# Joining the last two stores of a matmul with RMS norm into one, from one wide tile

## The chip, the cores and the metric

The kernel runs on one core of a Trainium2 chip. The metric is the device time of one execution in microseconds (us), as the median over runs; smaller is better. Beside the total I use a second figure, **the tail**: the time from the start of the last reciprocal (the instant when the last row block's 1/rms is being made) to the end of the profiled span. Times "after r" in this document are counted from the start of that reciprocal. The profile's pages round to 0.01 or 0.1 us; where I give the end of a packet or the landing of a store after r, it is from the trace's records of single packets and semaphore updates.

Three words recur. A store is *issued* by an instruction on SP or ACT; the 16 DMA engines then move it in *packets*, here one for each contiguous piece of a row; it has *landed* when its last semaphore update arrives. A run counts as "fast" unless it lies 1.5% above the fastest of the same kernel.

## The reference

```python
def reference(a, b, gamma, eps):            # a, b: 2048 x 2048 fp32, gamma: 2048
    x = np.matmul(a, b)
    rms = np.sqrt(np.mean(x ** 2, axis=-1, keepdims=True) + eps)
    return (gamma * x / rms).astype(np.float32)
```

A row of the output can only be finished when the whole row of the product is there, for rms needs its sum of squares.

## The kernel before

The kernel computes the product in bf16 and fp16 with Strassen's seven products per pair of row blocks. A row block has 128 rows, a row four chunks of `CH` = 512 columns (2 KB each in fp32); `HALF` is 1024, `N` and `K` are 2048. The last pair of row blocks is `ra`, `rb`; the part that matters here is the end of `last_group`, where block `rb` is finished. DVE is VectorE, ACT ScalarE, SP the engine that only issues here.

```python
        right = a_pool.tile([P, K], FP32, name="a32")[:, 0:HALF]
        add(right[:, 0:CH], p4[1], gam[2], ALU.mult)      # chunk 2 times gamma, out of PSUM (DVE)
        add(x22[0], seed, gam[1], ALU.mult)               # chunk 1 times gamma; x22[0] is xb[:, CH:]
        # [...] the last 16 matmuls (chunk 3 in two halves), their squares, the sum of squares
        r_b = inverse_rms(half_sq[:, 1:2], part)          # ACT: square root, DVE: reciprocal
        nc.vector.tensor_scalar_mul(out=xb[:, 0:CH], in0=xb[:, 0:CH], scalar1=r_b)   # chunk 0
        nc.sync.dma_start(out=rows(rb, 0, CH), in_=xb[:, 0:CH])
        by_r(right[:, 0:CH], r_b)                         # chunk 2, on ACT
        for bank, col in zip(half, halves):               # chunk 3, on DVE, out of PSUM
            scaled_gamma(right[:, CH:][:, col], bank, r_b, gam[3][:, col])
        nc.sync.dma_start(out=rows(rb, HALF, N), in_=right)        # chunks 2 and 3: 512 KB
        by_r(xb[:, CH:], r_b)                             # chunk 1, on ACT
        nc.scalar.dma_start(out=rows(rb, CH, HALF), in_=xb[:, CH:])   # chunk 1: 256 KB
```

So block `rb` leaves in three stores: chunk 0 early, then chunks 2 and 3 from SP's queue in rows of 4 KB, and chunk 1 from ACT's queue in rows of 2 KB.

Of the kernel before, what the change touches and what calls it, by code (L numbers as in the profile page):

```python
# [8 lines left out]
FP32 = mybir.dt.float32  # L9
# [4 lines left out]
ALU = mybir.AluOpType  # L14
# [3 lines left out]
def kernel(  # L18
# [13 lines left out]
    nc = tc.nc  # L32
    P = 128
    M, K = a.shape
    _, N = b.shape
# [4 lines left out]
    CH = 512  # L40
    NCH = N // CH
    HALF = N // 2
# [6 lines left out]
    a_pool = ctx.enter_context(tc.tile_pool(name="a_pool", bufs=2))  # L49
# [42 lines left out]
    for h, queue in enumerate((nc.sync, nc.scalar)):  # L92
        queue.dma_start(out=a0f[:, 2 * h:2 * h + 2, :],
                        in_=a[2 * h * P:(2 * h + 2) * P, 0:W2].rearrange("(r p) k -> p r k", p=P))
# [16 lines left out]
    a32 = {}  # L111
# [201 lines left out]
    def x_tile(mb, h):  # L313


        if (mb, h) not in x_half:
            n = n_x[0]
            n_x[0] += 1
            if n < 8:
                slot = n  # L320
            else:
                g = n // 4
                slot = ((0, 4, 1, 5), (0, 1, 4, 5))[g // 2 % 2 == 0][n % 4] + 2 * (g % 2)
            x_half[mb, h] = x_slot[slot]
        return x_half[mb, h]

    def x_chunk(mb, c):
        return x_tile(mb, c // 2)[:, (c % 2) * CH:(c % 2 + 1) * CH]
# [26 lines left out]
    def inverse_rms(last, partial):  # L355
        return inverse(root(last, partial))

    def rows(mb, lo, hi):
        return out[mb * P:(mb + 1) * P, lo:hi]
# [159 lines left out]
    x11, x12, x21, x22 = (x_chunk(r, c) for r in (r2, r3) for c in (2, 3))  # L519
# [185 lines left out]
    def last_group():  # L705
# [3 lines left out]
        ra, rb = 2 * g, 2 * g + 1  # L709
        x11, x12, x21, x22 = ([x_chunk(mb, 2 * j + c) for j in range(2)]  # L710
                              for mb in (ra, rb) for c in range(2))
        xa, xb = x_tile(ra, 0), x_tile(rb, 0)
        gam = [gamma_sb[:, c * CH:(c + 1) * CH] for c in range(NCH)]
# [3 lines left out]
        def partial(mb):  # L717

            m = msq[mb]
            part = stat_pool.tile([P, 1], FP32, name="part")  # L720
            nc.vector.tensor_scalar(out=part, in0=m[:, 0:1], scalar1=m[:, 1:2],
                                    scalar2=m[:, NCH:], op0=ALU.add, op1=ALU.add)
            return part
# [6 lines left out]
        def add(out, in0, in1, op=ALU.add):  # L730
            nc.vector.tensor_tensor(out=out, in0=in0, in1=in1, op=op)  # L731

        def scaled_gamma(x, src, r, gamma_of_x):
            nc.vector.scalar_tensor_tensor(out=x, in0=src, scalar=r, in1=gamma_of_x,
                                           op0=ALU.mult, op1=ALU.mult)

        def by_r(x, r):
            nc.scalar.activation(out=x, in_=x, func=ACTF.Copy, scale=r)  # L738

        p4 = []  # L740
        for j in range(2):
# [22 lines left out]
            if j == 0:  # L764
# [3 lines left out]
                seed = p7  # L768
# [19 lines left out]
        nc.sync.dma_start(out=rows(ra, CH, HALF), in_=mid)  # L788
        square(rb, seed)
        pre_b = partial(rb)  # L790
        right = a_pool.tile([P, K], FP32, name="a32")[:, 0:HALF]
        add(right[:, 0:CH], p4[1], gam[2], ALU.mult)
        add(x22[0], seed, gam[1], ALU.mult)

        half_sq = stat_pool.tile([P, 2], FP32, name="n2")
        part = stat_pool.tile([P, 1], FP32, name="part")
# [10 lines left out]
        r_b = inverse_rms(half_sq[:, 1:2], part)  # L807
        nc.vector.tensor_scalar_mul(out=xb[:, 0:CH], in0=xb[:, 0:CH], scalar1=r_b)
        nc.sync.dma_start(out=rows(rb, 0, CH), in_=xb[:, 0:CH])
        by_r(right[:, 0:CH], r_b)  # L810
        for bank, col in zip(half, halves):
            scaled_gamma(right[:, CH:][:, col], bank, r_b, gam[3][:, col])
        nc.sync.dma_start(out=rows(rb, HALF, N), in_=right)
        by_r(xb[:, CH:], r_b)
        nc.scalar.dma_start(out=rows(rb, CH, HALF), in_=xb[:, CH:])

    for g in range(G0, NG - 1):
        for j in range(2):
            group_half(g, j, hooks_of(g, j))
    last_group()  # L820

# [33 lines left out]
```

## Time and profile before

| | before |
|---|---|
| time, median of the first 3 runs | 221.2 us (221.19 to 221.22) |
| span of the profiled run | 219.0 us |
| end of the last matmul | 211.96 us |
| start of the last reciprocal | 212.89 us |
| tail, from there to the end of the span | 6.11 us |

TensorE is busy for 95% of the span, nearly to its end, and the tail is a chain of its own: reciprocal, scaling, issue, transfer, confirmation, closing waits. Only the tail can answer to this change. The lines are shown and read in the prediction below.

### The profile page before, as it was taken

Reading aid. Unit: us, or ns where it says so; the run is one execution under the profiler, and the core shown is the slowest. Engines: PE = TensorE matmul, PEld = TensorE weight load, DVE = VectorE, ACT = ScalarE, POOL = GpSimd, SP = SyncE. Lnnn points to the kernel's source line nnn. Section 1 sums busy time; section 2 is a strip of 40 time slices with the busy share of each in tenths; the row PEclk is TensorE's granted clock in tenths of the full one; section 3 lists DMA queues with packets and bytes.
Section 4 is the critical chain, followed back from the end, with each engine's and each line's share of the span. In section 5 each row is a group of like instructions: output and inputs, shape, how many; then the busy total and the mean of one; then the engine's idle time right before and its main releaser. Section 6 shows DMA issues by size and latency. Waiting matters only on the chain.

```text
span 219.0 us, 3023 instructions
## 1 busy us (share of the span) xinstructions
PE 208.8 (95%) x1012; PEld 98.4 (45%) x1032; DVE 165.9 (76%) x326; ACT 127.0 (58%) x263; POOL 36.2 (17%) x75
## 2 busy tenths in 40 slices
PE   7999999999999999999999999999999999999970
PEld 3544544444455444444444444444444444444440
DVE  1228799999899998988794649856794759787781
ACT  2110002920599898788646996289747996334471
POOL 7644433433020002100200002000200000000040
PEclk9999999999999999999999999999999999999996
DMA  7999999999939698939899049955799349145045
GB/s 152 175 202 206 204 206 209 210 208 224 414 91 332 232 278 214 379 153 263 213 294 381 19 87 272 355 233 96 174 291 396 57 89 365 69 178 208 1 179 206
DMA packets 36864, 46.60 MB, mean 213 GB/s; under 512 B 22256, under 2 KB 26352, under 8 KB 35568
## 3 DMA queue, kind: packets, MB, share of 16 engines
q0 software_dynamic: 10608, 23.86, 44.3%
q1 hardware_dynamic: 25824, 22.02, 33.4%
q10 hardware_dynamic: 416, 0.52, 0.7%
q8 instruction: 8, 0.13, 0.2%
q14 instruction: 8, 0.07, 0.1%
HBM read 34.60 MB, written 16.78 MB: 235 GB/s over the span
## 4 chain that ended last, share of the span: by engine, by line
PE 91%; DMA 3%; issue 1%; ACT 1%; POOL 1%; DVE 0%; ACTq 0%; POOLq 0%
PE acc L285 71%; PE acc L388 16%; DMA early<-in_a_dram 3%; PE tbank L419 2%; PE tbank L168 2%; PE acc L799 1%; POOL b L102 0%; PE tbank L185 0%; PE acc L185 0%; ACT x L738 0%; DVE head_at L173 0%; ACT sq L802 0%; ACT rms L352 0%; POOL t_left masks.py:199 0%; POOL t_left masks.py:197 0%
## 5 line engine op out<-in xcount | busy, mean ns | idle before, releaser
L285 PE MATMUL acc<-b,s 128*128 128x512 bf16 x397 | 92.7, 379 | 0.7
L285 PEld LDWEIGHTS <-s 128*128 128x128 f16 (+1 forms) x512 | 50.0, 98 | 59.6 <-DVE s L260 0.2
L388 PE MATMUL acc<-b,head_at 128*128 128x512 bf16 x171 | 42.2, 379 | 0.4 <-DMA b<-in_b_dram 0.3
L303 ACT ACTIVATE sq<-x 128x512 bf16<-128x512 f32 x53 | 33.4, 630 | 6.9 <-DVE x L731 3.0
L370 DVE SCALAR_TENSOR_TENSOR x<-x,r,gamma_sb 128x1024 f32<-128x1024 f32 x28 | 34.9, 1281 | 0.7
L219 ACT ACTIVATE sq<-a 128x1024 bf16<-128x1024 f32 x24 | 25.3, 1053 | 2.0 <-DMA a<-in_a_dram 1.4
L388 PEld LDWEIGHTS <-head_at 128*128 128x128 bf16 x176 | 16.9, 98 | 19.5 <-issue 0.7
L242 ACT ACTIVATE head_at<-a,s 128x2048 f16<-128x2048 f32 x10 | 20.0, 1998 | 3.4 <-DVE s L229 3.3
L102 POOL DMA_DIRECT2D b<-in_b_dram x32 | 17.2, 540 | 20.4 <-DMA b<-in_b_dram 14.1
L430 ACT COPY x<-acc 128x512 f32<-128x512 f32 x5 | 2.9, 582 | 24.6 <-PE acc L388 24.6
L285 PEld LDWEIGHTS <-head_at 128*128 128x128 f16 (+1 forms) x112 | 11.0, 98 | 13.2
L285 PEld LDWEIGHTS <-at_even 128*128 128x128 f16 x96 | 9.4, 98 | 11.3
L285 PE MATMUL acc<-early,head_at 128*128 128x512 bf16 x63 | 14.4, 379 | 0.1
L285 PE MATMUL acc<-early,s 128*128 128x512 bf16 x56 | 14.2, 379 | 0.0
L260 DVE TENSOR_TENSOR s<-head_at 128x1024 f16<-128x1024 f16 (+5 forms) x22 | 13.4, 636 | 0.1
L615 DVE TENSOR_TENSOR x<-x,x 128x512 f32<-128x512 f32 x9 | 6.2, 692 | 8.8 <-ACT x L613 8.3
L127 POOL COPY pace<-x 128x1 f32<-128x1 f32 x4 | 1.7, 413 | 66.3 <-DVE x L624 65.0
L597 ACT COPY x<-acc 128x512 f32<-128x512 f32 x9 | 5.2, 573 | 11.5 <-PE acc L285 7.7
L285 PE MATMUL acc<-t_left,s 128*128 128x512 bf16 x47 | 11.3, 379 | 0.1
L783 POOL TENSOR_SCALAR x<-x,r 128x512 f32<-128x512 f32 x1 | 2.7, 2653 | 51.2 <-DVE r L346 51.2
L276 DVE TENSOR_TENSOR b<-b 128x1024 bf16<-128x1024 bf16 x16 | 10.8, 686 | 0.2
L173 DVE COPY head_at<-tbank 128x1024 bf16<-128x1024 bf16 x7 | 4.8, 692 | 8.0 <-PE tbank L168 7.9
(113 smaller groups left out, 239.3 us busy)
## 6 DMA issues: line engine op xcount, KB each, us to landing
out_dram<-x SPq DMA_DIRECT2D x29, 512.0 KB, 3.7
a<-in_a_dram POOLq DMA_DIRECT2D x10, 1024.0 KB, 8.6
b<-in_b_dram POOLq DMA_DIRECT2D x32, 256.0 KB, 9.9
a<-in_a_dram POOLq DMA_DIRECT2D x4, 512.0 KB, 9.8
early<-in_a_dram POOLq DMA_DIRECT2D x7, 256.0 KB, 10.0
gamma_sb<-in_gamma_dram POOLq DMA_DIRECT2D x2, 512.0 KB, 8.3
out_dram<-x SPq DMA_DIRECT2D x3, 256.0 KB, 2.6
out_dram<-a SPq DMA_DIRECT2D x1, 512.0 KB, 3.3
```

What stands on the lines that cost most here:

```text
L102: nc.gpsimd.dma_start(out=raw[j][kp][:, t, :], in_=b[lo:lo + P, j * HALF:(j + 1) * HALF])
L173: nc.vector.tensor_copy(out=head_at[:, 2 * kp:2 * kp + 2, :, :], in_=view)
L219: nc.scalar.activation(out=junk, in_=a32[mb][:, h * HALF:(h + 1) * HALF], func=ACTF.Square, scale=2.0 ** -8, accum_out=n2[:, h:h + 1])
L242: nc.scalar.activation(out=a16[mb], in_=a32.pop(mb), func=ACTF.Copy, scale=factor.pop(mb))
L260: nc.vector.tensor_tensor(out=sum_of(g, s)[:, lo:hi, :], in0=x[:, lo:hi, :], in1=y[:, lo:hi, :], op=op)
L276: nc.vector.tensor_tensor(out=flat[:, 1:3, :], in0=flat[:, 1:3, :], in1=flat[:, 0::3, :], op=ALU.add)
L285: nc.tensor.matmul(bank, lhsT[:, kp, :], rhs, start=(start and kp == 0), stop=(kp == KP - 1), skip_group_check=not start)
L303: nc.scalar.activation(out=sq[:, 0:CH], in_=src, func=ACTF.Square, scale=inv_sqrt_n, accum_out=msq[mb][:, c:c + 1])
L370: nc.vector.scalar_tensor_tensor(out=x, in0=x, scalar=inverse_of[mb], in1=gamma_sb[:, h * HALF:(h + 1) * HALF], op0=ALU.mult, op1=ALU.mult)
L388: nc.tensor.matmul(bank, head_at[:, kt, r, :], head_rhs(c, kt), start=(kt == 0), stop=(kt == KT - 1))
L597: nc.scalar.copy(out=c, in_=one[1])
L615: nc.vector.tensor_tensor(out=t, in0=t, in1=x12, op=ALU.add)
```

## The change

The intent: chunk 1's product with gamma goes into the same wide tile as chunks 2 and 3, side by side with them, so that the three leave together as one store of 768 KB, each row a single packet of 6 KB. One issue, one semaphore and half of the packets are saved.

```diff
-        right = a_pool.tile([P, K], FP32, name="a32")[:, 0:HALF]
-        add(right[:, 0:CH], p4[1], gam[2], ALU.mult)
-        add(x22[0], seed, gam[1], ALU.mult)
+        wide = a_pool.tile([P, K], FP32, name="a32")
+        chunk = [wide[:, c * CH:(c + 1) * CH] for c in range(NCH)]
+        add(chunk[2], p4[1], gam[2], ALU.mult)
+        add(chunk[1], seed, gam[1], ALU.mult)
 [...]
-        by_r(right[:, 0:CH], r_b)
+        for c in (2, 1):
+            by_r(chunk[c], r_b)
         for bank, col in zip(half, halves):
-            scaled_gamma(right[:, CH:][:, col], bank, r_b, gam[3][:, col])
-        nc.sync.dma_start(out=rows(rb, HALF, N), in_=right)
-        by_r(xb[:, CH:], r_b)
-        nc.scalar.dma_start(out=rows(rb, CH, HALF), in_=xb[:, CH:])
+            scaled_gamma(chunk[3][:, col], bank, r_b, gam[3][:, col])
+        nc.sync.dma_start(out=rows(rb, CH, N), in_=wide[:, CH:])
```

## The prediction

> **What bounds the kernel now.** I read the page first: the chain that ended last, then the timeline of the last ten microseconds, the DMA issues there, and that stretch cut into windows, in this order.
>
> The chain that ended last, as shares of the span by engine:
>
> ```profile
> PE 91%; DMA 3%; issue 1%; ACT 1%; POOL 1%; DVE 0%; ACTq 0%; POOLq 0%
> ```
>
> Nine tenths of the 219.0 us span are TensorE (PE) work, one matmul after the other. The change touches no matmul, so this part stays. What it touches is the tail behind the last matmul, which ends at 211.97. The timeline there (start, duration, engine, line, operation, count; SPq and ACTq are DMA issues by the two queues):
>
> ```profile
> 212.89 0.16 DVE L346 RECIPROCAL r<-rms 128x1 f32<-128x1 f32 x1 [0.50 <-ACT rms L352]
> 213.08 0.72 ACT L738 ACTIVATE a<-a,r 128x512 f32<-128x512 f32 x1 [0.23 <-DVE r L346]
> 213.09 0.49 DVE L808 TENSOR_SCALAR x<-x,r 128x512 f32<-128x512 f32 x1
> 213.49 0.87 DVE L734 SCALAR_TENSOR_TENSOR a<-acc,r,gamma_sb 128x256 f32<-128x256 f32 x2
> 213.60 0.33 SPq L809 DMA_DIRECT2D out_dram<-x  x1
> 213.71 0.70 ACT L738 ACTIVATE x<-x,r 128x512 f32<-128x512 f32 x1
> 214.42 0.33 SPq L813 DMA_DIRECT2D out_dram<-a  x1
> 214.45 0.36 ACTq L815 DMA_DIRECT2D out_dram<-x  x1
> ```
>
> The reader is to see four chunks of 512 columns being multiplied by 1/rms (`r`), which is there at 213.05. DVE does chunk 0 (until 213.58), which is stored at once by L809. Then DVE does chunk 3 in two halves, until 213.49 + 0.87 = 214.36. ACT does chunk 2 (until 213.80) and then chunk 1 (until 214.41). Chunks 2 and 3 go out together from SP at 214.42 (L813, 512 KB), chunk 1 from ACT's queue at 214.45 (L815, 256 KB). **Both last stores leave within 0.03 us of each other.** No compute instruction follows.
>
> What follows is pure transfer. The DMA issues of the last eleven microseconds, with the median time from issue to landing, are:
>
> ```profile
> out_dram<-a SPq DMA_DIRECT2D x1, 512.0 KB, 3.3
> out_dram<-x ACTq DMA_DIRECT2D x1, 256.0 KB, 3.5
> ```
>
> So L813 lands at about 214.42 + 3.3 = 217.7 and L815 at 214.45 + 3.5 = 217.95; the second ends the kernel's work, and some 1.05 us of closing waits on SP bring the span to 219.0. The windows show what the DMA engines did (busy columns, then granted clock, DMA share, GB/s):
>
> ```profile
> 214.50:215.00 0.50, 0.00 (x0) 0.00 (x0) 0.00 (x0) 0.00 (x0) 0.00 (x0) 0.92 1.00 381
> 215.00:215.50 0.50, 0.00 (x0) 0.00 (x0) 0.00 (x0) 0.00 (x0) 0.00 (x0) 0.50 0.87 316
> 215.50:216.00 0.50, 0.00 (x0) 0.00 (x0) 0.00 (x0) 0.00 (x0) 0.00 (x0) 0.50 0.97 381
> 216.00:216.50 0.50, 0.00 (x0) 0.00 (x0) 0.00 (x0) 0.00 (x0) 0.00 (x0) 0.50 1.06 422
> 216.50:217.00 0.50, 0.00 (x0) 0.00 (x0) 0.00 (x0) 0.00 (x0) 0.00 (x0) 0.50 0.98 373
> 217.00:217.50 0.50, 0.00 (x0) 0.00 (x0) 0.00 (x0) 0.00 (x0) 0.00 (x0) 0.50 0.53 185
> ```
>
> A share near 1 means that all 16 engines are moving data. Up to about 215.1 they move chunk 0, from about 215.2 to 217.3 the 768 KB of the other three. The tail is a bandwidth stretch with a start-up ahead of it and a confirmation behind it (217.3 to 217.95). And the packets of 215.2 to 217.4 by queue (q1 is SP's, q10 is ACT's; packets, MB, share of 16 engines' time):
>
> ```profile
> q1 hardware_dynamic: 152, 0.52, 61.1%
> q10 hardware_dynamic: 143, 0.26, 31.6%
> ```
>
> From this comes the price of a packet. The window holds 2.2 x 16 = 35.2 engine-us. q1: 0.611 x 35.2 = 21.5 us over its 128 packets of 4 KB (the other 24 carry next to nothing) is 168 ns each. q10: 0.316 x 35.2 = 11.1 us over 128 packets of 2 KB is 87 ns each. So 2 KB more cost 81 ns more, and the part that does not scale with size is only about 6 ns.
>
> **What the Trainium skill says.**
> - "DMA: Bandwidth & Descriptors", section "Issuing engines are not separate DMA queues": DMAs started from several engines share the same 16 DMA engines and interleave; a second issuer only saves issue time. The trace agrees: both queues' packets share 215.6 to 217.3, and the total stays near 400 GB/s.
> - Same page, "Why small descriptors are slow (HBM only)": a fixed overhead of about 3 cycles per packet, and joining descriptors is worth it only at 256 B or below. The 6 ns of 87 agree: at 2 KB there is little left to win.
> - Same page, "Anatomy of one DMA — SWDGE (gpsimd) path": fitted, one DMA takes about 2.0 us plus bytes over 436e3 per us. That is for the software path, yet for 256 KB it gives 2.6 us, where the three 256 KB stores of SP had a median of 2.6, and 3.2 for 512 KB, where the two stores took 3.1 and 3.3.
> - "Perfetto Trace Analysis", section "DMA Instruction — HWDGE (DVE, Sync)": the last descriptor bumps the semaphore only when the write is confirmed, which can be long when the target is HBM. Here 0.6 us pass between the last packets (217.3) and the landing (217.95).
>
> **The change, part by part.**
> 1. The destination of chunk 1's gamma product moves from `x22[0]` into the same wide tile that holds chunks 2 and 3. It is the same DVE instruction (L731, 0.68 us at 211.52), between the last squares, with the same operands and shape. The wide tile is the buffer that was already allocated, whole, and used by half. Cost: 0.
> 2. ACT's two scalings (0.72 and 0.70 us) come in the same order, chunk 2 then 1; DVE's two halves of chunk 3 likewise. They write other columns of one tile; in the kernel before, DVE's chunk 3 and ACT's chunk 2 already did so at the same time (DVE starts at 213.49 while ACT runs until 213.80), so sharing a tile makes no wait. Cost: 0.
> 3. The store of chunks 2 and 3 no longer leaves when DVE is done (214.36) but when ACT is done as well (214.41). SP follows its releaser by 0.02 to 0.06 us here (L809 issues 0.02 after DVE's 213.58, L813 0.06 after 214.36), so it issues at 214.44 to 214.47 instead of 214.42. Cost: +0.02 to +0.05 us on the path, the only thing the merge can delay.
> 4. One issue of 0.36 us on ACT goes. It ran beside SP's 0.33 us and ended before the data moved. Its packets came late, though: L815 issued at 214.45 and the first packets of q10 are seen only after 215.6, while those of SP began near 215.2. But the engines were busy with q1 meanwhile, so this cost nothing. Gain: 0.
> 5. The packets. Before, each of the 16 engines moves 8 packets of 4 KB and 8 of 2 KB: 8 x (168 + 87) = 2.04 us. After, 8 of 6 KB. An estimate from the line through the two measured sizes is 6 + 3 x 81 = 249 ns, so 8 x 249 = 1.99 us. Gain: 0.05 us; perhaps 0.1 if part of the spread of packet times was the two queues switching.
> 6. The end. Two landings become one, on one semaphore. The confirmation of 0.6 us stays, as do the closing waits of 1.05 us. Gain: 0, or a few hundredths.
>
> Sum: +0.03 - 0.05 to - 0.10, and perhaps - 0.05 from the end: **about -0.1 us**, so 221.2 becomes 221.1.
>
> **The rivals.**
> - *The merge delays a store that could have left early.* This would cost, had chunk 3 been ready well before chunk 1. The timeline speaks against it: 214.36 against 214.41. Worth +0.05 at most, counted above.
> - *Two queues kept the engines fuller than one.* With one queue, its packets have nothing to interleave with. Chunk 0 alone on SP moved at 381 GB/s at share 1.00 (214.5 to 215.0), the pair at 373 to 422. So one queue is enough; if 6 KB packets were 5% worse, +0.1 us.
> - *A bigger DMA has its own fixed cost.* The skill's fit gives 2.0 + 786432/436e3 = 3.8 us for 768 KB, which would land at 214.45 + 3.8 = 218.25, 0.3 later than now: 221.5. Against it: part of the measured 3.3 us of L813 was time spent on the other queue's packets, so the two-queue landing of 3.5 us already holds all 768 KB.
> - *The larger packets win more.* If the half microsecond at 316 GB/s (215.0 to 215.5) was the hand-over to two queues, one long transfer would fill it: (381 - 316) x 0.5 = 33 KB, or 0.09 us at 381 GB/s. That would give 221.0. But the hand-over is from chunk 0 to the next store, and it stays.
>
> **Range and chances.** The working gives 221.1; the rivals reach from 221.0 to 221.5. The runs before spread only 0.03 us, so noise adds little: 220.8 to 221.4 should hold eight times in ten. Two per cent are 4.4 us. From `r` (213.05) to the end are 5.95 us, most of which is a transfer of unchanged bytes, so a gain of that size has no room, and a loss of that size would need the transfer of 2 us to triple.
>
> **What would show it.** In the changed kernel's trace: nothing from ACT's queue at the end (q10 loses 256 KB); the first and second ACT scalings of the tail still back to back, DVE unchanged beside them; one 768 KB issue by SP within 0.05 us of the end of the second scaling (step 3); packets of some 249 ns, 128 of them, done about 2.0 us after they start (step 5); landing some 3.4 us after issue, and about 1.05 us to the end (step 6). The prediction is wrong if 6 KB rows are cut into small packets or move at a clearly other rate, if sharing the tile makes ACT or DVE wait for each other, or if the landing of one large store is confirmed later than that of two.

## The result, and the profile after

| | before | after |
|---|---|---|
| median of the runs of the same rounds | 221.18 us (220.88 to 221.22, 6 runs) | 220.94 us (220.72 to 221.36, 6 runs) |
| ratio after to before | | 0.9992, 95% interval 0.9979 to 1.0005 |
| span of the profiled run | 219.0 us | 219.1 us |
| tail of the profiled run | 6.11 us | 5.98 us |

A ratio here is the mean time of one kernel's fast runs over that of the other's fast runs of the same rounds, so it is not quite the ratio of the two medians. The interval holds 1. The totals don't resolve a tenth of a microsecond; the profiled run of the changed kernel even has the longer span, because its last reciprocal started 0.26 us later (213.15 instead of 212.89), as its last matmul had already ended 0.26 us later (212.22 instead of 211.96). The tail does resolve it.

The timeline of the changed kernel behind the last matmul (start, duration, engine, line, operation, count):

```profile
213.15 0.16 DVE L346 RECIPROCAL r<-rms 128x1 f32<-128x1 f32 x1 [0.50 <-ACT rms L352]
213.35 1.33 ACT L738 ACTIVATE a<-a,r 128x512 f32<-128x512 f32 x2 [0.23 <-DVE r L346]
213.35 0.49 DVE L809 TENSOR_SCALAR x<-x,r 128x512 f32<-128x512 f32 x1
213.75 0.87 DVE L734 SCALAR_TENSOR_TENSOR a<-acc,r,gamma_sb 128x256 f32<-128x256 f32 x2
213.86 0.33 SPq L810 DMA_DIRECT2D out_dram<-x  x1
214.71 0.33 SPq L815 DMA_DIRECT2D out_dram<-a  x1
```

Against the kernel before, every compute instruction stands at the same distance from the reciprocal: ACT starts 0.20 us after it and now shows its two scalings as one group of two (1.33 us, until 214.68), DVE starts 0.20 and 0.60 us after it. The ACT queue's issue is gone. The one merged issue comes at 214.71, which is 1.56 us after r; L813 came at 214.42 - 212.89 = 1.53.

The DMA issue and, for 215.5 to 217.7, the packets of the merged store (packets, MB, share of 16 engines' time):

```profile
out_dram<-a SPq DMA_DIRECT2D x1, 768.0 KB, 3.3
```
```profile
q1 hardware_dynamic: 146, 0.79, 88.2%
```

The window holds 2.2 x 16 = 35.2 engine-us; 0.882 of it over 128 packets of 6 KB (the other 18 carry next to nothing) is 243 ns each; the records of the 128 packets alone give 241. The windows (busy columns, clock, DMA share, GB/s):

```profile
215.00:215.50 0.50, 0.00 (x0) 0.00 (x0) 0.00 (x0) 0.00 (x0) 0.00 (x0) 1.00 0.84 303
215.50:216.00 0.50, 0.00 (x0) 0.00 (x0) 0.00 (x0) 0.00 (x0) 0.00 (x0) 1.00 0.96 393
216.00:216.50 0.50, 0.00 (x0) 0.00 (x0) 0.00 (x0) 0.00 (x0) 0.00 (x0) 1.00 0.98 406
216.50:217.00 0.50, 0.00 (x0) 0.00 (x0) 0.00 (x0) 0.00 (x0) 0.00 (x0) 0.67 1.03 418
217.00:217.50 0.50, 0.00 (x0) 0.00 (x0) 0.00 (x0) 0.00 (x0) 0.00 (x0) 0.50 0.90 356
```

This is the same picture as before: a dip around 215.5 (around 215.25 in the kernel before) where chunk 0 has nearly ended and the next store has hardly begun, then about 400 GB/s until the data runs out. Nothing was removed from this stretch but packets.

### The profile page after: what moved, and what is told of

It reads as the page before. It is cut to its first block, busy times and chain, and to the rows that moved or that the text cites. A ratio compares the mean times of both kernels' runs of the same rounds, so it can differ in the third digit from the quotient of the medians.

```text
span 219.1 us, 3041 instructions
## 1 busy us (share of the span) xinstructions
PE 209.2 (95%) x1032; PEld 97.7 (45%) x1032; DVE 165.9 (76%) x326; ACT 127.0 (58%) x263; POOL 36.4 (17%) x75
## 4 chain that ended last, share of the span: by engine, by line
PE 92%; DMA 3%; ACT 1%; POOL 1%; issue 1%; DVE 0%; ACTq 0%; POOLq 0%
PE acc L285 71%; PE acc L388 16%; DMA early<-in_a_dram 3%; PE tbank L419 2%; PE tbank L168 2%; PE acc L800 1%; POOL b L102 0%; PE acc L185 0%; PE tbank L185 0%; ACT a L738 0%; DVE head_at L173 0%; ACTq L850 0%; ACT sq L803 0%; ACT rms L352 0%; POOL t_left masks.py:199 0%
## 5 line engine op out<-in xcount | busy, mean ns | idle before, releaser
L388 PE MATMUL acc<-b,head_at 128*128 128x512 bf16 x176 | 43.0, 379 | 1.2 <-DMA b<-in_b_dram 0.8
L303 ACT ACTIVATE sq<-x 128x512 bf16<-128x512 f32 x53 | 33.4, 630 | 6.9 <-DVE x L731 3.0
```

What stands on the lines that cost most here:

```text
L303: nc.scalar.activation(out=sq[:, 0:CH], in_=src, func=ACTF.Square, scale=inv_sqrt_n, accum_out=msq[mb][:, c:c + 1])
L388: nc.tensor.matmul(bank, head_at[:, kt, r, :], head_rhs(c, kt), start=(kt == 0), stop=(kt == KT - 1))
```

## The experiments

Eleven runs, all correct. This table holds what each showed; the texts below refer to it. All columns but the last are us after r. "Data" is the first packet of the last store (or of the last pair of stores) and the end of the last packet; "landed" is the last semaphore update of a store; the tail is the end of the span.

| run | last stores, packets | last issue | data | landed | tail | median total |
|---|---|---|---|---|---|---|
| before, first trace | 512 KB of 4 KB + 256 KB of 2 KB, two queues | 1.56 | 2.38 to 4.52 | 5.01 | 6.11 | 221.18 |
| before_again | the same | 1.56 | 2.38 to 4.52 | 4.99 | 6.09 | 220.98 |
| after, first trace | 768 KB of 6 KB | 1.56 | 2.40 to 4.47 | 4.90 | 5.98 | 220.94 |
| after_again | the same | 1.56 | 2.40 to 4.47 | 4.90 | 6.01 | 220.95 |
| after_third | the same | 1.56 | 2.40 to 4.47 | 4.90 | 5.98 | 220.90 |
| wide_two_queues | as before | 1.56 | 2.38 to 4.52 | 5.00 | 6.09 | 221.13 |
| wide_two_on_sp | as before, both from SP | 1.96 | 2.38 to 4.51 | 5.30 | 6.34 | 221.54 |
| one_store_2k | 768 KB of 2 KB | 1.56 | 2.46 to 4.67 | 5.01 | 6.10 | 221.36 |
| one_store_1k | 768 KB of 1 KB | 1.56 | 2.47 to 4.90 | 5.25 | 6.33 | 221.64 |
| whole_row | 1 MB of 8 KB, nothing ahead of it | 1.56 | 2.39 to 5.05 | 5.41 | 6.57 | 221.86 |
| chunk1_early | 256 KB of 2 KB, then 512 KB of 4 KB | 1.62 | ends 4.74 | 5.22 | 6.27 | 221.25 |
| chunk1_early_again | the same | 1.63 | ends 4.72 | 5.20 | 6.25 | 221.16 |
| pool_helps | 768 KB of 6 KB | 1.63 | 2.46 to 4.52 | 4.90 | 6.51 | 221.67 |

My theory going in was the prediction's: the compute and the issue are as before, and the small gain is that of larger packets. The rivals: the layout itself does it, the second queue does it, or the number of landings does it.

**after_again.** The changed kernel, unaltered.

> The changed kernel once more, to see how well its tail repeats. The tail is taken as the time from the start of the last reciprocal (r) to the end of the span: 6.10 us before, 5.98 us after in the first traces. If the tail is a property of the program and the rest of the spread lies in front of it, this run gives 5.98 within 0.03 us, whatever the total. If the tail itself is noisy by 0.1 us or more, the 0.12 us between the first two traces means nothing.

Tail 6.01 us against 5.98, and a last landing at 4.90 us both times, though its whole span was 219.5 us instead of 219.1. So the tail belongs to the program, and the spread of the totals arises before r. The tail can be used to 0.03 us.

**wide_two_queues.** The tile of the change, the stores of before.

```diff
-        for c in (2, 1):
-            by_r(chunk[c], r_b)
+        by_r(chunk[2], r_b)
         [chunk 3 on DVE]
-        nc.sync.dma_start(out=rows(rb, CH, N), in_=wide[:, CH:])
+        nc.sync.dma_start(out=rows(rb, HALF, N), in_=wide[:, HALF:])
+        by_r(chunk[1], r_b)
+        nc.scalar.dma_start(out=rows(rb, CH, HALF), in_=chunk[1])
```

> The wide tile alone: chunks 1 to 3 side by side, but the stores as before (512 KB from SP, 256 KB from ACT's queue). My theory (the tile costs nothing, the whole gain is in the merged store): tail 6.10 us as before, within 0.03. Rival (the layout itself changes something, by a wait between engines that write one tile or by where the tile lies): tail near 5.98 or above 6.15.

Tail 6.09 us, and data and landing as in the kernel before to 0.01 us. The layout costs and wins nothing; the rival of the layout falls. All of the gain is in the store.

**wide_two_on_sp.** As the last one, but chunk 1's store is issued by SP too (`nc.scalar` becomes `nc.sync` in the last line).

> Two stores as before, but both from SP's queue: the second queue is gone, the merge is not made, packets stay 4 KB and 2 KB. Packet theory (gain comes from fewer, larger packets): 8 x (0.160 + 0.086) = 1.97 us of data instead of 8 x 0.241 = 1.93, so tail 6.02 to 6.15, and the later issue of the second store (at some 214.8 in the clock of before) is hidden behind the first one's data. Queue theory (gain comes from not using a second queue, whose packets came 0.4 us after SP's and were slowed): tail 5.98 to 6.02, as after.

A miss for both theories: tail 6.34 us, longer than either kernel. The end of the data is as before (4.51 us against 4.52), so the second queue had cost the data nothing, as the packet theory has it; but the landing took 0.79 us from there, against 0.49 before and 0.43 after. The issues show what changed:

```profile
215.02 0.33 SPq L814 DMA_DIRECT2D out_dram<-a  x1
215.44 0.41 SPq L816 DMA_DIRECT2D out_dram<-a  x1
```
```profile
out_dram<-a SPq DMA_DIRECT2D x1, 512.0 KB, 2.8
out_dram<-x SPq DMA_DIRECT2D x1, 256.0 KB, 2.6
out_dram<-a SPq DMA_DIRECT2D x1, 256.0 KB, 3.3
```

The second store is issued 0.42 us behind the first (215.44 against 215.02) although its data was ready at the same time (0.33 us of that are the first issue itself), and it lands 3.3 us later, at 1.96 + 3.34 = 5.30 us after r. That a later issue on one queue is confirmed so much later, when its packets ended on time, I had not expected and can't explain from these runs. It does show that giving up the second queue is not by itself a gain: without the merge it is a loss of 0.24 us.

**one_store_2k.** One store as in the change, but the chunks lie 64 bytes apart in the tile, so that every row leaves in three packets of 2 KB.

```diff
-        chunk = [wide[:, c * CH:(c + 1) * CH] for c in range(NCH)]
+        PAD = CH + 16
+        parts = wide[:, 0:3 * PAD].rearrange("p (c n) -> p c n", n=PAD)[:, :, 0:CH]
+        chunk = [None] + [parts[:, c, :] for c in range(3)]
 [...]
-        nc.sync.dma_start(out=rows(rb, CH, N), in_=wide[:, CH:])
+        nc.sync.dma_start(out=rows(rb, CH, N).rearrange("p (c n) -> p c n", n=CH), in_=parts)
```

> One store of 768 KB as in the change, but the three chunks lie 64 bytes apart in the tile, so that it goes out in 2 KB packets: one issue, one queue, one landing, 3 x 128 packets. Packet theory: 8 x 3 x 0.086 = 2.06 us of data against 1.93, tail 0.13 to 0.16 longer than after, 6.11 to 6.14. Queue or landing theory: tail 5.98 as after, for the number of stores is what counts.

Tail 6.10 us: as long as before, though the store is still one. The packet theory expected 6.11 to 6.14, the rivals of the queue and of the number of landings 5.98. The packets of 216.2 to 218.6 in this run, and the issue:

```profile
q1 hardware_dynamic: 401, 0.79, 87.1%
```
```profile
215.40 0.38 SPq L817 DMA_DIRECT2D out_dram<-a  x1
```

0.871 x 2.4 x 16 = 33.4 engine-us over 384 packets is 87 ns each. Each engine moves 24 of them: 2.09 us, against 8 x 0.241 = 1.93 us.

That the tail equals that of before is in part a coincidence, for three things differ from the change. The issue takes 0.38 us instead of 0.33, and the first packet comes at 2.46 instead of 2.40: +0.06. From the first packet to the last it takes 2.20 us instead of 2.07: +0.13, as reckoned. The landing comes 0.35 us behind the last packet instead of 0.43: -0.08. Only the second is the price of the packets. Nor does the run refute that the number of stores or landings counts: from the first packet to the last landing this one store took 2.55 us with 384 packets, the two stores of before 2.62 us with 256, and the change 2.49 to 2.50 us with 128.

**one_store_1k.** The same with six pieces of 1 KB, for a second point (`PAD = CH // 2 + 16`, six parts; two per chunk).

> One store of 768 KB again, now in 1 KB packets (six pieces, 64 bytes apart). A second point for the price of a packet. The first runs gave 6 KB: 241 ns, 4 KB: 164, 2 KB: 87, so about 78 ns per 2 KB and 8 to 10 ns per packet; 1 KB packets then take 46 to 48 ns and the data 8 x 6 x 0.047 = 2.26 us against 1.93 of the change: the last packet ends 0.3 us later. If the end of the data sets the tail alone: 6.30. If the confirmation behind it gets shorter again, as it did with 2 KB packets in one store (0.35 us against 0.43), 6.15 to 6.25.

Tail 6.33 us. The data ended at 4.90 us, 0.43 later than in the change and more than the 0.3 expected, 0.07 of it because it began later (2.47 instead of 2.40, behind an issue of 0.38 us again); the confirmation was 0.35 us again. The packets of 215.8 to 218.4:

```profile
q1 hardware_dynamic: 784, 0.79, 88.8%
```

0.888 x 2.6 x 16 = 36.9 engine-us over 768 packets is 48 ns each. Three sizes in one store give tails of 5.98 (6 KB), 6.10 (2 KB) and 6.33 (1 KB), but the issue, the start and the confirmation differ too. What follows the size of the packets is the stretch from the first to the last: 2.07, 2.20 and 2.42 us.

**whole_row.** The merge driven to the end: chunk 0 in the tile as well, one store of 1 MB.

```diff
-        nc.vector.tensor_scalar_mul(out=xb[:, 0:CH], in0=xb[:, 0:CH], scalar1=r_b)
-        nc.sync.dma_start(out=rows(rb, 0, CH), in_=xb[:, 0:CH])
+        nc.vector.tensor_scalar_mul(out=chunk[0], in0=xb[:, 0:CH], scalar1=r_b)
 [...]
-        nc.sync.dma_start(out=rows(rb, CH, N), in_=wide[:, CH:])
+        nc.sync.dma_start(out=rows(rb, 0, N), in_=wide)
```

> The merge driven further: chunk 0 too goes into the tile and all four leave as one store of 1 MB in 8 KB packets, at some 1.56 us after the start of r instead of 0.71 for chunk 0. Rival of the prediction (a merge costs when it holds back a part that was ready early): chunk 0's data, which otherwise runs from 1.5 to 2.4 us after r, now comes behind the issue: data from 2.40 to 2.40 + 8 x 0.315 = 4.92, against 4.47, tail 6.35 to 6.5. If instead fewer and larger packets are what counts, tail below 5.98.

Tail 6.57 us, 0.58 longer than the mean of the three traces of the change (5.99) and 0.07 above the range expected, though its packets are the largest of all. The issue and the start of its data are nearly those of the change (1.56 and 2.39, against 1.56 and 2.40), but chunk 0's 256 KB now lie behind that point instead of ahead of it. This is the prediction's first rival made true on purpose: a merge costs what a part that was ready early is held back. In the change next to nothing was: DVE had chunk 3 ready 1.47 us after r and ACT chunk 1 at 1.53.

**chunk1_early**, run twice. The opposite: a store more. ACT does chunk 1 first, it goes out alone, and chunks 2 and 3 follow as 512 KB.

```diff
-        for c in (2, 1):
-            by_r(chunk[c], r_b)
+        by_r(chunk[1], r_b)
+        nc.sync.dma_start(out=rows(rb, CH, HALF), in_=chunk[1])
+        by_r(chunk[2], r_b)
         [chunk 3 on DVE]
-        nc.sync.dma_start(out=rows(rb, CH, N), in_=wide[:, CH:])
+        nc.sync.dma_start(out=rows(rb, HALF, N), in_=wide[:, HALF:])
```

> Against the merge: three stores from SP, chunk 0 when DVE has it, chunk 1 when ACT has it (ACT does it first now), chunks 2 and 3 together as 512 KB. In the change the DMA engines run dry for some 0.15 us between the end of chunk 0 and the first packets of the merged store, which come 0.84 us after its issue. If that gap is what is left to win, chunk 1's packets fill it: the data ends near 1.5 + 8 x (0.087 + 0.087 + 0.164) = 4.2 to 4.3 us after r instead of 4.47, tail 5.75 to 5.9, shorter than both kernels though packets are smaller. If packet size and number of stores set the tail, it is as long as before or longer, 6.1 to 6.3.

> The three-store version again, because its first profile had a disturbed main part (the whole ran 1.3 us longer than the others before r) and its 4 KB packets took 185 ns instead of 164. If the packets' slowness belongs to that one execution, the data now ends at 4.25 to 4.35 us after r, and the tail is 5.75 to 5.95. If three stores close together are slow by themselves, the packets again take over 180 ns, the data ends near 4.7 and the tail is 6.2 to 6.3.

Both misses, and the second run shows that the first was not an accident: tails of 6.27 and 6.25 us, where filling the dip should have given 5.75 to 5.9. The dip is filled, but the packets got slower. Windows of 0.4 us in the second run, of which the first begins 2.04 us after r:

```profile
215.10:215.50 0.40, 0.00 (x0) 0.00 (x0) 0.00 (x0) 0.00 (x0) 0.00 (x0) 1.00 1.05 379
215.50:215.90 0.40, 0.00 (x0) 0.00 (x0) 0.00 (x0) 0.00 (x0) 0.00 (x0) 1.00 1.09 323
215.90:216.30 0.40, 0.00 (x0) 0.00 (x0) 0.00 (x0) 0.00 (x0) 0.00 (x0) 1.00 1.31 394
216.30:216.70 0.40, 0.00 (x0) 0.00 (x0) 0.00 (x0) 0.00 (x0) 0.00 (x0) 0.76 0.85 266
```

The four moved 379, 323, 394 and 266 GB/s, 340 on the mean, at a mean DMA share of 1.08: the engines are busy and move less than the 400 of the change. Single packets of 4 KB took up to 0.34 us in the first run, 0.185 on the mean, instead of 0.164. The late end has a second part: in the second run the number of packets under way fell from 15 to 2 between 4.20 and 4.65 us after r, where the change takes from 4.30 to 4.45. Why the engines moved less and ended so unevenly, these runs don't show. So the dip of the change, which looked like 0.15 us to be won, is not to be had by keeping the engines fed in this way.

**pool_helps.** The change, with 128 of chunk 2's columns scaled by GpSimd (POOL), so that ACT is done sooner.

```diff
-        for c in (2, 1):
-            by_r(chunk[c], r_b)
+        cut = CH - P
+        nc.gpsimd.tensor_scalar_mul(out=chunk[2][:, cut:], in0=chunk[2][:, cut:], scalar1=r_b)
+        by_r(chunk[2][:, 0:cut], r_b)
+        by_r(chunk[1], r_b)
```

> The change with 128 of chunk 2's 512 columns scaled by GpSimd instead of ACT, so that ACT is done some 0.1 us earlier and the merged store leaves when DVE is done: issue at 1.47 to 1.50 us after r instead of 1.56. If the issue of the last store sets the end (0.84 us later its packets start), tail 5.98 - 0.06 to - 0.09 = 5.89 to 5.92. If GpSimd needs more than 1.2 us for it (its 512 columns took 2.65 us earlier on) or slows DVE, tail 6.0 or more.

A miss on both sides. ACT and POOL were done in time, but the issue came later, not sooner:

```profile
213.15 1.23 ACT L738 ACTIVATE a<-a,r 128x384 f32<-128x384 f32 x2 [0.23 <-DVE r L346]
213.20 0.90 POOL L812 TENSOR_SCALAR a<-a,r 128x128 f32<-128x128 f32 x1 [1.04 <-DVE r L346]
213.55 0.87 DVE L734 SCALAR_TENSOR_TENSOR a<-acc,r,gamma_sb 128x256 f32<-128x256 f32 x2
214.58 0.33 SPq L817 DMA_DIRECT2D out_dram<-a  x1
```

DVE ended at 214.42, ACT at 214.38, POOL at 214.10, and SP issued at 214.58, 0.16 us behind the last of them instead of the 0.03 us of the change. (The profile's spans of GpSimd are rough, so POOL may have been done later than it shows.) Even so the store landed 4.90 us after r, as in the change, though its data ended 0.05 us later (4.52): the landing does not follow the last packet by a fixed time. The tail is 6.51 us because the closing waits on SP grew. In the change and in this run they are:

```profile
SPq L850 <- PEq L850: 0.7, 2, 0.5
```
```profile
SPq L852 <- PEq L852: 1.2, 2, 0.7
```

0.5 us more (total, times, longest) pass between the landing and the end when GpSimd has worked in the tail. The trace's records show what is waited for: a DRAIN instruction of GpSimd at the end of the program. In all thirteen traces it ended 4.58 us after GpSimd's last scaling. In the change that scaling ended 0.78 us before r and the DRAIN 3.80 us after it, long before SP had done its own last waits (5.22). Here the scaling ended at 1.15, so the DRAIN ended at 5.74 and the rest of the close came behind it. What takes the 4.58 us is not shown.

**after_third and before_again.** Both kernels unaltered, on the chip of the second chunk1_early run.

> The changed kernel on the same chip as the run above, for a fair comparison: tail 5.98 to 6.01 as in both of its profiles so far, last landing 4.90 us after r.

> The kernel before, profiled once more, on the same chip: tail 6.09 to 6.10, last landing 5.00 to 5.01 us after r, as in its first profile and in that of the wide tile with two queues. If it lies below 6.03, the difference of 0.1 us to the changed kernel is not settled.

Tails of 5.98 and 6.09 us. So the change has 5.98, 6.01, 5.98, on the mean 5.99 us, and the kernel before has 6.11 and 6.09 us, on the mean 6.10; the layout with the old stores gave 6.09. The difference of 0.11 us is several times the spread, and it shows on one chip in the same rounds. The totals, on the other hand, can't tell it: in these rounds the ratio of the change to the kernel before was 0.9983 (0.9964 to 1.0003), and that of the kernel before to itself 0.9982 (0.9962 to 1.0002).

No version beat the change in the tail.

## Why the prediction was right

It said 221.1 us (220.8 to 221.4), within 2%, by a gain of 0.1 us. Measured were 220.94 us and a tail that is 0.11 us shorter. That the median fell into the range is partly luck: the prediction held that noise adds little, from three runs that spread 0.03 us, but the six runs of the changed kernel spread 0.64 us, more than the range is wide. The totals' own difference of medians in the first rounds, 0.24 us, is no better confirmation than 0.1 would have been, since the same kernel run against itself in the last rounds gave a ratio of 0.9982.

The sum came out better than its terms. As written they add up to a gain of 0.02 to 0.12 us, and "about 0.1" took the favourable end. Measured, from the means of the two traces of before and the three of the change: the data starts 0.02 us later, its stretch is 0.07 shorter, the confirmation is 0.06 shorter, and the closing waits are the same. So the step on the end, expected to give nothing or a few hundredths, made up half of the gain.

Point by point:

1. *The new place of chunk 1's product costs nothing.* Right: wide_two_queues has the tail of before.
2. *The scalings on ACT and DVE are unchanged and don't wait for each other.* Right: all start at the same distances from r.
3. *The issue comes 0.02 to 0.05 us later.* Right: 1.559 us after r against 1.534 for L813. The first packet follows by the same amount, 2.40 against 2.38.
4. *Taking away ACT's issue gains nothing by itself.* Right for the data: with the second queue gone and the packets as before (wide_two_on_sp) the data ends at 4.51 us, against 4.52. For the landing it is open: no run has one store with the packets of before.
5. *Larger packets gain 0.05 us.* Right: the data ended 0.05 us earlier (4.52 to 4.47), and with the start 0.02 us later the stretch from first to last packet shrank by 0.07. A packet of 6 KB took 241 ns, not the 249 estimated. The 168 ns for 4 KB held the small packets of the window too (the 4 KB packets alone give 166), and in one queue (wide_two_on_sp) it is 164; the part that doesn't scale with size is about 9 ns, not 6.
6. *The end gains nothing or a few hundredths.* Right, at the upper end: from the last packet to the last landing 0.43 us instead of 0.49. (The 0.6 us of the prediction was read from the windows; the records have the last packet at 217.41, not 217.3, and the landing at 217.90.) What sets this time is open. In the seven traces where one store goes out behind chunk 0, or alone, it is 0.35 to 0.43 us, with packets of 1 to 8 KB; in the six with two stores or three close together it is 0.47 to 0.79. So this half of the gain goes with the number of stores, but no run isolates that.

Of the rivals, the first is a real mechanism that this change does not meet: whole_row pays 0.58 us for holding back chunk 0. The second, that two queues keep the engines fuller, falls: one queue ran at 393 to 418 GB/s in the three full windows, two queues at 373 to 422. The third, that 768 KB would need 3.8 us from issue to landing, falls too: 4.90 - 1.56 = 3.34 us. The fourth, that the half microsecond around the hand-over could be won, is answered by the dip, which stays in the changed kernel as the prediction said.

## What to carry to other kernels

Before joining stores, compare the times at which their parts are ready: here, joining parts that were ready together cost 0.02 us and halved the packets, and joining a part that was ready early cost 0.58 us for its 256 KB. For 768 KB, rows of 6 KB instead of 2 KB were worth 0.13 us of transfer, and 0.35 instead of 1 KB; the bytes are the rest. A little work on GpSimd near the end can cost more than it saves: see when its last instruction ends. And a gain of a tenth of a microsecond is not to be read from totals: take the distance from the last event ahead of the change to the end of the span, and profile each kernel twice.

## What the Trainium skill lacked or had wrong

- "DMA: Bandwidth & Descriptors", section "Why small descriptors are slow (HBM only)", calls joining descriptors into one packet worth it only at 256 B or below. The prediction leaned on that, but the change is another thing, for its rows themselves become longer; for that the section gives no times. In stores of 128 rows issued by SP the mean packet took 48 ns at 1 KB, 87 at 2 KB, 164 at 4 KB and 241 at 6 KB: about 9 ns that don't scale with size, a tenth of a 2 KB packet. In 2 KB packets 768 KB took 0.13 us longer from first to last packet than in 6 KB packets.
- Same page, section "Anatomy of one DMA — SWDGE (gpsimd) path": the fit of 2.0 us plus bytes over 436e3 is for DMAs issued by GpSimd. For stores issued by SP the estimate from it held at 256 KB (2.6 us) and at 512 KB (3.1 and 3.3 us measured, 3.2 estimated) in the kernel before, but was too long for the larger ones: 3.34 us measured for 768 KB (3.8 estimated), and 5.41 - 1.56 = 3.85 us for 1 MB (4.4 estimated). The page has no fit for that path.
- For a store issued by SP no page that I read says how long the confirmation behind the last packet is: 0.35 to 0.79 us here, by the shape and the order of the stores. "Perfetto Trace Analysis", section "DMA Instruction — HWDGE (DVE, Sync)", only calls it surprisingly long.
- No page that I read says how long GpSimd's last DRAIN takes: it ended 4.58 us after GpSimd's last scaling in all thirteen traces, and in pool_helps this put 0.5 us on the end.
